# Grouped-query attention on one core: five of sixteen exps on VectorE, one of them as a pair summed on GpSimd

## The chip, the core and the metric

The kernel runs on one core of a Trainium2 chip. The core has engines that run side by side, each with its own queue of instructions: TensorE (PE, matrix multiplications, with its weight loads shown as PEld), VectorE (DVE), ScalarE (ACT), GpSimd (POOL) and SyncE (SP, which here only issues transfers). An instruction starts when those ahead of it on its engine have been issued and the semaphores it waits for are reached. Matrix products land in PSUM, eight banks of 2 KB per partition; everything else lies in SBUF. The metric is the device time of one execution in microseconds.

## The reference

Attention with 32 query heads and 8 key/value heads, batch 8, sequence 512, head size 64; four query heads share one key/value head.

```python
Q = Q.transpose(0, 2, 1, 3)
K_expanded = K_expanded.transpose(0, 2, 1, 3)
V_expanded = V_expanded.transpose(0, 2, 1, 3)
scores = np.einsum('bhqd,bhkd->bhqk', Q, K_expanded) * scale
weights = np.exp(scores - np.max(scores, axis=-1, keepdims=True))
weights = weights / (np.sum(weights, axis=-1, keepdims=True) + 1e-10)
output = np.einsum('bhqk,bhkd->bhqd', weights, V_expanded)
return output.transpose(0, 2, 1, 3).astype(np.float32)
```

## The kernel before

A unit is one batch entry and two key/value heads with their eight query heads; there are 32. A unit has 16 score tiles, four for each of four pairs of query heads. One score tile (`mm_scores`) is two matmuls of 64x128 weights against 64x512 queries, the two halves of the array at work on one head each, into a tile of two PSUM banks. There are three such slots, so PE can be ahead of the exps by three tiles. Two further banks, the x tiles, serve transposes and output blocks in turn.

The exps have no maximum subtracted. Most run on ACT (`exp_act`, one instruction for 128x1024). Some run on DVE (`exp_dve`): the score is multiplied and shifted so that, converted to a 16-bit integer, its bits are those of a bf16 number near the exponential (Schraudolph's method). The table `TILES` marks by a 1 the tiles of a unit that go to DVE, four of sixteen here. A 2 marks a tile whose bits go to a tile `lo` instead; GpSimd then makes a second copy `hi`, half an octave up (64 added to each 16-bit number), and adds the two as bf16 into the probability tile `pt`, so that the errors of the two approximations partly cancel. In the kernel before no tile is marked 2.

The output (`mm_out`) is made in blocks of four matmuls, 128 keys each, with V and a column of ones, so that column 64 of a block holds the sum of the weights. A unit has 32 blocks; DVE copies them out of PSUM in groups (`take_out`, tile `raw`). When a unit is whole, DVE takes the reciprocal of the sums, GpSimd multiplies (`divide`), and SP stores. Q, K and V are loaded as bf16 by GpSimd's queue; K and Q are transposed by PE (`mm_turn`) and copied out by DVE (`take_turn`, tiles `kt` and `qt`), and two transfers on SP make a copy of `kt` with its halves swapped, which the second head of a score tile needs.

The order of all this is written out ahead by the class `Plan`, with a cost for each kind of work. `SCORES` says for each of 16 places in a unit whether the score tile made there is one for ACT or for DVE; `FILL` says how many blocks or transposes PE does after each place; `ORDER` is the sequence of these (K4 the four transposes of K, 08 and 18 eight transposes of the first and the second half of Q, o7 seven output blocks); `SKIP` shifts that sequence against the places. The output blocks of a unit are made while the next unit's scores are. DVE takes what is ready first by the plan's costs. `fix` is the time that the plan allows for the work on GpSimd behind a tile marked 2.

```python
TILES = [int(c) for c in "0100010001000100"]
SCORES = "ADAADAADAAADAAAA"
FILL = [0, 0, 13, 0, 0, 7, 0, 0, 6, 0, 7, 0, 4, 0, 0, 15]
ORDER = "o4 o7 K4 08 18 o7 o7 o7".split()
```

Of the kernel before, what the change touches and what calls it, by code (L numbers as in the profile page):

```python
# [11 lines left out]
BF16 = mybir.dt.bfloat16  # L12
U8 = mybir.dt.uint8
U16 = mybir.dt.uint16
PE = mybir.EngineType.PE
ACT = mybir.EngineType.Activation
DVE = mybir.EngineType.DVE
# [5 lines left out]
class Plan:  # L23
# [11 lines left out]
    SCH, SCH_VIS = 1.14, 1.277  # L35
    DRAIN = 0.1

    def __init__(self, nu, tiles, scores, fill, groups, skip, arrive, x_cost, fix, nslot, nx, npt):
        self.ops = []
        qa = [16 * u + t for u in range(nu) for t in range(16) if not tiles[t]]  # L40
        qd = [16 * u + t for u in range(nu) for t in range(16) if tiles[t]]
        pt, pair_done, parts = {}, {}, {(0, None): 0.0, (0, 0): 0.0}
        slots, xs = [0.0] * nslot, [0.0] * nx
        ready = []
        self.pe = self.act = self.dve = 0.0
        ia = id_ = gi = at = nxt = 0
        scoring = False
        carry = -skip

        def run_dve(until):  # L50
            while ready:
                j = min(ready, key=lambda j: (max(j[0] - self.dve, 0.0), j[0]))
                start = max(self.dve, j[0])
                if start > until:
                    return
                ready.remove(j)
                self.ops.append((start, "dve", j[1], j[2]))
                if j[1] == "score":
                    cost, vis = self.SCH, self.SCH_VIS
                    slots[j[3]] = start + vis  # L60
                    pt[j[2]] = start + vis + (fix if tiles[j[2] % 16] == 2 else 0.0)
                else:
                    cost, vis = x_cost(j[2])
                    xs[j[3]] = start + vis
                    if j[1] == "turn":
                        swap = 4.0 if j[2][2] is None else 0.0
                        parts[j[2][1:3]] = start + vis + swap
                self.dve = start + cost

        def step_dve():  # L70
            assert ready
            run_dve(min(max(self.dve, j[0]) for j in ready) + 1e-9)

        def known(d, key):
            while d[key] >= NEVER if isinstance(d, list) else key not in d:
                step_dve()
            return d[key]

        for u in range(nu + 3):
            for k in range(16):  # L80
                at_dve = scores[k] == "D"
                if (id_ < len(qd)) if at_dve else (ia < len(qa)):
                    t = qd[id_] if at_dve else qa[ia]
                    p = t // 4
                    start = self.pe + (0.0 if scoring else self.DRAIN)
                    run_dve(start)
                    start = max(start, known(parts, (p // 4, None)), known(parts, (p // 4, p % 4 // 2)))
                    assert p < npt or p - npt in pair_done
                    while True:
                        s = min(range(nslot), key=lambda i: slots[i])  # L90
                        if ready and min(max(self.dve, j[0]) for j in ready) < max(start, slots[s]):
                            step_dve()
                        elif slots[s] >= NEVER:
                            step_dve()
                        else:
                            break
                    self.pe = max(start, slots[s])
                    scoring = True
                    slots[s] = NEVER
                    self.ops.append((self.pe, "pe", "score", (t, s)))  # L100
                    if at_dve:
                        ready.append((self.pe + self.SCORE_LAT, "score", t, s))
                        id_ += 1
                    else:
                        start = max(self.act, self.pe + self.SCORE_LAT)
                        self.ops.append((start, "act", "score", t))
                        self.act = start + self.EXP
                        slots[s] = pt[t] = start + self.EXP_VIS
                        ia += 1
                    self.pe += self.SCORE  # L110
                carry += fill[k]
                loose = u < 1 or u >= nu - 2
                while carry > 0 and gi < len(groups):
                    f = groups[gi]
                    start = self.pe + (self.DRAIN if scoring else 0.0)
                    run_dve(start)
                    limit = start + 0.1 if loose and u < nu else NEVER
                    if at == 0:
                        while xs[nxt % nx] >= NEVER:
                            step_dve()  # L120
                        start = max(start, xs[nxt % nx])
                    if f[0] == "turn":
                        start = max(start, arrive(f))
                    else:
                        p = f[1] * 4 + (f[2] + at) // 8
                        if p * 4 + 3 >= 16 * nu or any(
                            t not in pt and t not in [j[2] for j in ready if j[1] == "score"]
                            for t in range(4 * p, 4 * p + 4)
                        ):
                            assert loose  # L130
                            break
                        start = max([start] + [known(pt, t) for t in range(4 * p, 4 * p + 4)])
                    if start > limit:
                        break
                    self.pe = start
                    scoring = False
                    self.ops.append((start, "pe", f[0], (f, at)))
                    self.pe += self.TURN if f[0] == "turn" else self.BLOCK
                    carry -= 1
                    if at == 0:  # L140
                        x = nxt % nx
                        xs[x] = NEVER
                        nxt += 1
                    at += 1
                    if f[0] == "out" and (f[2] + at) % 8 == 0:
                        pair_done[p] = self.pe
                    if at == f[3]:
                        ready.append((self.pe + self.X_LAT, f[0], f, x))
                        gi, at = gi + 1, 0
                carry = min(carry, 16)  # L150
        run_dve(NEVER)
        assert ia == len(qa) and id_ == len(qd) and gi == len(groups)
        self.ops = [o for _, o in sorted(enumerate(self.ops), key=lambda e: (e[1][0], e[0]))]
# [3 lines left out]
def kernel(  # L157
# [7 lines left out]
    nc = tc.nc  # L165

    B, S, H, D = Q.shape
# [11 lines left out]

    TILES = [int(c) for c in "0100010001000100"]
    SCORES = "ADAADAADAAADAAAA"
    FILL = [0, 0, 13, 0, 0, 7, 0, 0, 6, 0, 7, 0, 4, 0, 0, 15]
    ORDER = "o4 o7 K4 08 18 o7 o7 o7".split()
    SKIP = 9

    scale = 1.0 / math.sqrt(D)
    A_schr = (2.0 ** 7) / math.log(2.0) * scale
# [82 lines left out]
    def exp_dve(t):  # L272
# [11 lines left out]
        )  # L284
        if two:
            high = two_pool.tile([128, 2, S], U16, name="hi")
            nc.gpsimd.tensor_scalar(
                out=high, in0=bits, scalar1=HALF_OCTAVE, scalar2=None, op0=mybir.AluOpType.add
            )
            nc.gpsimd.tensor_tensor(  # L290
                out=dst, in0=bits.bitcast(BF16), in1=high.bitcast(BF16), op=mybir.AluOpType.add
# [18 lines left out]
    def take_out(f, now):  # L310
# [11 lines left out]
        for a, b in ((0, 2 * BLK), (2 * BLK, 3 * BLK)) if last else (  # L322
            (0, 2 * BLK), (2 * BLK, UB)
        ) if u == NU - 2 else ((0, UB),):
            if lo < b <= lo + n:
                divide(u, a, b - a, nc.vector if last and a else nc.gpsimd)
                wait = 4.5 if b - a == UB else 2.8
                later.append((now + wait, lambda a=a, b=b: store(u, a, b - a, nc.sync)))

    def divide(u, lo, n, eng, src=None):  # L330
        src = raws[u][:, lo:lo + n, :] if src is None else src
        inv = inv_pool.tile([128, UB], FP32, name="inv")[:, 0:n]
        nc.vector.reciprocal(out=inv, in_=src[:, :, D])  # L333
        nh = n // SC
        eng.tensor_tensor(  # L335
            out=osbs[u].rearrange("p qc h d -> p h qc d")[:, lo // SC:lo // SC + nh],
            in0=src[:, :, 0:D].rearrange("p (h qc) d -> p h qc d", h=nh),
            in1=inv.rearrange("p (h qc) -> p h qc", h=nh)[:, :, :, None].to_broadcast(
                (128, nh, SC, D)
            ),  # L340
            op=mybir.AluOpType.mult,
        )

    def store(u, lo, n, eng):
        b, gp = divmod(u, GP)
# [33 lines left out]
                load_q(u + 3)  # L379

    turned = {}
    groups = [("turn", 0, 1, 8), ("turn", 1, None, 4), ("turn", 1, 0, 8), ("turn", 1, 1, 8)]
    for u in range(NU - 1):
        lo = 0
        for word in ORDER:
# [16 lines left out]
    def arrive(f):  # L402
        return {(0, 1): 0.5, (1, None): 3.0}.get(f[1:3], 6.0 if f[1] == 1 else 0.0)

    plan = Plan(
        NU, TILES, SCORES, FILL, groups, SKIP, arrive, x_cost,
        fix=5.0, nslot=NSLOT, nx=2, npt=6,
    )

    with tc.manual_schedule(engines={PE, ACT, DVE, POOL, SP}):  # L410
# [13 lines left out]
        v1f = first.tile([128, SC, 2, D1], BF16, name="v1f")  # L424
        nc.gpsimd.memset(v1f[:, :, :, D:D1], 1.0)
        v1[0] = v1f
        load_q(0, lo=HPG)
        load_k(0)
        load_q(1)
# [85 lines left out]
```

## Time and profile before

| | |
|---|---|
| time, median of 3 runs | 370.14 us (369.25 to 370.32) |
| profiled execution | 370.1 us, its span 368.2 us |
| ACT busy | 355.6 us, 97% |
| PE busy (ends modelled) | 341.9 us, 93% |
| DVE busy | 304.2 us, 83% |
| POOL busy | 167.1 us, 45% |
| DMA | 64.41 MB, mean 175 GB/s |
| granted TensorE clock | 0.995 |

The span runs from the first to the last instruction in the trace. A busy share is an average over the span; a busy time counts an instruction until its result has landed, and the next one on the engine can begin a little earlier, so that summed times can exceed what the engine needs. In the rows of the timeline stand start, duration, engine, line, operation, output and input tiles, and in brackets how long the engine was idle ahead of it and what ended that.

### The profile page before, as it was taken

What the parts mean: (1) busy time and instruction counts of PE and PEld (TensorE: products, weight loads), DVE (VectorE), ACT (ScalarE), POOL (GpSimd) and SP (SyncE); (2) the same over time, 40 slices, a digit from 0 to 9 for tenths busy, and PEclk for the clock granted to TensorE, in tenths of its full rate; (3) what the DMA queues carried; (4) which work ended last, traced back from release to release, by engine and by line L of the source; (5) the groups of instructions that cost most, each with busy time, mean ns of one, the idle gap of its engine ahead of it and who ended that gap; (6) DMA issues with size and microseconds to landing.
All of it is one profiled execution on the core that took longest, in us unless ns stands there. A gap on an engine that the chain in (4) does not pass through costs nothing.

```text
span 368.2 us, 13048 instructions
## 1 busy us (share of the span) xinstructions
PE 341.9 (93%) x5774; PEld 220.6 (60%) x5774; DVE 304.2 (83%) x430; ACT 355.6 (97%) x387; POOL 167.1 (45%) x105
## 2 busy tenths in 40 slices
PE   8799999999999999999999999999999999999993
PEld 3366566666565666566656566656666656666652
DVE  3788888888888888888888888898888898988883
ACT  4999999999999999999999999999999999999993
POOL 5334642446444264642436454254643436333161
PEclk9999999999999999999999999999999999999998
DMA  8999667797669966698865967879657995712355
GB/s 186 207 204 208 147 127 173 141 254 224 138 123 230 247 158 154 140 207 206 188 169 94 255 176 173 187 168 261 162 113 162 213 264 143 169 55 98 129 202 144
DMA packets 51480, 64.41 MB, mean 175 GB/s; under 512 B 3424, under 2 KB 36064, under 8 KB 51424
## 3 DMA queue, kind: packets, MB, share of 16 engines
q0 software_dynamic: 25344, 24.91, 42.8%
q1 hardware_dynamic: 25024, 38.28, 33.0%
q8 instruction: 45, 0.74, 0.8%
q10 hardware_dynamic: 1056, 0.39, 0.4%
q14 instruction: 11, 0.09, 0.1%
HBM read 50.86 MB, written 33.55 MB: 229 GB/s over the span
## 4 chain that ended last, share of the span: by engine, by line
PE 47%; ACT 34%; DVE 12%; DMA 2%; issue 2%; POOL 0%; ACTq 0%; DVEq 0%; POOLq 0%
ACT pt L265 34%; PE x L301 27%; DVE pt L277 11%; DMA k_nat<-in_K_dram 2%; DVE raw L321 0%; PE x L362 0%; DVE o_sb L335 0%; POOL q_nat L222 0%; ACTq L265 0%; PE s_2568 L254 0%; DVEq L277 0%; DVE inv L333 0%; PE s_344 L254 0%; PE s_6778 L254 0%; PE s_6531 L254 0%
## 5 line engine op out<-in xcount | busy, mean ns | idle before, releaser
L335 POOL TENSOR_TENSOR o_sb<-raw,inv 128x2048 f32<-128x2048 f32 (+1 forms) x33 | 114.1, 3458 | 183.4 <-issue 135.8
L301 PEld LDWEIGHTS <-pt 128*128 128x128 bf16 x4096 | 134.3, 98 | 40.2 <-issue 39.4
L321 DVE COPY raw<-x 128x455 f32<-128x455 f32 (+1 forms) x161 | 93.5, 581 | 45.7 <-PE x L301 45.7
L254 PEld LDWEIGHTS <-kt 64*128 64x128 bf16 x1024 | 51.1, 93 | 81.1 <-issue 54.8
L376 DVE COPY qt<-x 128x1024 bf16<-128x1024 bf16 x63 | 42.9, 681 | 0.7 <-PE x L362 0.7
L362 PE MATMUL x<-ident,q_nat 128*128 128x128 bf16 x504 | 39.2, 220 | 0.1
L362 PEld LDWEIGHTS <-q_nat 128*128 128x128 bf16 x504 | 28.3, 98 | 15.6 <-issue 15.2
L222 POOL DMA_DIRECT2D q_nat<-in_Q_dram x32 | 25.6, 801 | 0.1
L301 PE MATMUL x<-v_6732,pt 128*128 128x65 bf16 x512 | 18.9, 194 | 0.8 <-ACT pt L265 0.7
L301 PE MATMUL x<-v_5749,pt 128*128 128x65 bf16 x512 | 19.0, 194 | 0.0
L301 PE MATMUL x<-v_2800,pt 128*128 128x65 bf16 x512 | 19.0, 194 | 0.0
L301 PE MATMUL x<-v_3783,pt 128*128 128x65 bf16 x512 | 19.0, 194 | 0.0
L301 PE MATMUL x<-v_1817,pt 128*128 128x65 bf16 x512 | 19.0, 194 | 0.0
L301 PE MATMUL x<-v_4766,pt 128*128 128x65 bf16 x512 | 19.0, 194 | 0.0
L301 PE MATMUL x<-v_834,pt 128*128 128x65 bf16 x512 | 19.0, 194 | 0.0
L301 PE MATMUL x<-v_182,pt 128*128 128x65 bf16 x384 | 14.2, 194 | 0.0
L369 DVE COPY kt<-x 128x512 bf16<-128x512 bf16 x31 | 12.8, 414 | 0.0
L333 DVE RECIPROCAL inv<-raw 128x32 f32<-128x32 f32 (+2 forms) x34 | 11.6, 341 | 1.2
L362 PE MATMUL x<-ident,k_nat 128*128 128x128 bf16 x124 | 12.2, 219 | 0.4 <-DMA k_nat<-in_K_dram 0.4
L362 PEld LDWEIGHTS <-k_nat 128*128 128x128 bf16 x124 | 7.4, 97 | 1.0 <-DMA k_nat<-in_K_dram 0.5
L234 POOL DMA_DIRECT2D v_nat<-in_V_dram x8 | 6.1, 761 | 0.0
L229 POOL DMA_DIRECT2D k_nat<-in_K_dram x8 | 6.0, 751 | 0.0
(1068 smaller groups left out, 809.1 us busy)
## 6 DMA issues: line engine op xcount, KB each, us to landing
out_dram<-o_sb SPq DMA_DIRECT2D x30, 1024.0 KB, 5.6
q_nat<-in_Q_dram POOLq DMA_DIRECT2D x31, 512.0 KB, 8.4
k_nat<-in_K_dram POOLq DMA_DIRECT2D x8, 512.0 KB, 10.5
v_nat<-in_V_dram POOLq DMA_DIRECT2D x8, 512.0 KB, 12.4
kt<-kt SPq DMA_DIRECT2D x62, 64.0 KB, 2.0
out_dram<-o_sb SPq DMA_DIRECT2D x3, 512.0 KB, 3.8
q_102<-in_Q_dram ACTq DMA_DIRECT2D x1, 256.0 KB, 4.4
k_103<-in_K_dram SPq DMA_DIRECT2D x1, 256.0 KB, 3.9
```

The costliest lines, as they stand in the source:

```text
L222: nc.gpsimd.dma_start(out=t[:, :, lo * D:], in_=rows(Q, b, HU * gp + lo, HU * (gp + 1)))
L234: nc.gpsimd.dma_start(out=t, in_=rows(V, b, 0, KV))
L254: nc.tensor.matmul(s[:, m, :], kt[u][64 * m:64 * m + 64, 0 if m == g else 1, kc * 128:(kc + 1) * 128], qt[u][64 * m:64 * m + 64, i, :], st ...
L265: nc.scalar.activation(out=pts[p][:, kc, :, :], in_=score.pop(t), func=mybir.ActivationFunctionType.Exp, scale=float(scale),)
L277: nc.vector.tensor_scalar(out=bits, in0=score.pop(t), scalar1=float(A_schr), scalar2=float(B_two if two else B_one), op0=mybir.AluOpType.mult,
L301: nc.tensor.matmul(xs[f][:, at * D1:(at + 1) * D1], pts[u * HPG + i][:, kc, m, qc * 128:(qc + 1) * 128], v1[u][:, kc, 2 * i // HPG, :], st ...
L321: nc.vector.tensor_copy(out=raws[u][:, lo:lo + n, :], in_=x[:, 0:n * D1])
L333: nc.vector.reciprocal(out=inv, in_=src[:, :, D])
L335: eng.tensor_tensor(out=osbs[u].rearrange("p qc h d -> p h qc d")[:, lo // SC:lo // SC + nh], in0=src[:, :, 0:D].rearrange("p (h qc) d -> ...
L362: nc.tensor.transpose(xs[f][:, at * 128:(at + 1) * 128], src, ident)
L369: nc.vector.tensor_copy(out=k[:, 0, :], in_=x[:, 0:S])
L376: nc.vector.tensor_copy(out=qt[u][:, 2 * part:2 * part + 2, :], in_=x)
```

## The change

One more tile of each unit goes to DVE, as a pair (the 2 in `TILES`, tile 11); the tables of the order are new, with K's transposes first; `hi` is made by an add of 32-bit integers, each holding two 16-bit numbers, against a constant tile `shift`; a whole unit's division is made in two halves; and some constants of the plan differ.

```diff
-    TILES = [int(c) for c in "0100010001000100"]
-    SCORES = "ADAADAADAAADAAAA"
-    FILL = [0, 0, 13, 0, 0, 7, 0, 0, 6, 0, 7, 0, 4, 0, 0, 15]
-    ORDER = "o4 o7 K4 08 18 o7 o7 o7".split()
-    SKIP = 9
+    TILES = [int(c) for c in "0100010001020100"]
+    SCORES = "DAADAADAAADAADAA"
+    FILL = [0, 8, 0, 0, 13, 0, 0, 8, 0, 0, 9, 6, 0, 0, 8, 0]
+    ORDER = "K4 o7 08 o7 o6 18 o7 o5".split()
+    SKIP = 21
...
             high = two_pool.tile([128, 2, S], U16, name="hi")
-            nc.gpsimd.tensor_scalar(
-                out=high, in0=bits, scalar1=HALF_OCTAVE, scalar2=None, op0=mybir.AluOpType.add
+            nc.gpsimd.tensor_tensor(
+                out=high.rearrange("p m s -> p (m s)").bitcast(I32),
+                in0=bits.rearrange("p m s -> p (m s)").bitcast(I32),
+                in1=shift,
+                op=mybir.AluOpType.add,
             )
...
-                wait = 4.5 if b - a == UB else 2.8
+                wait = 5.0 if b - a == UB else 2.8
                 later.append((now + wait, lambda a=a, b=b: store(u, a, b - a, nc.sync)))
...
-        nh = n // SC
-        eng.tensor_tensor(
-            out=osbs[u].rearrange("p qc h d -> p h qc d")[:, lo // SC:lo // SC + nh],
...
+        parts = 2 if n == UB else 1
+        for part in range(parts):
+            nh = n // SC // parts
+            h0 = nh * part
+            eng.tensor_tensor(
+                out=osbs[u].rearrange("p qc h d -> p h qc d")[:, lo // SC + h0:lo // SC + h0 + nh],
...
-    groups = [("turn", 0, 1, 8), ("turn", 1, None, 4), ("turn", 1, 0, 8), ("turn", 1, 1, 8)]
+    groups = [("skip", 2), ("turn", 0, 1, 8), ("skip", 4), ("turn", 1, None, 4)]
+    groups += [("skip", SKIP - 6), ("turn", 1, 0, 8), ("turn", 1, 1, 8)]
...
-        fix=5.0, nslot=NSLOT, nx=2, npt=6,
+        fix=6.0, nslot=NSLOT, nx=2, npt=6,
...
+        shift = const.tile([128, S], I32)
+        nc.gpsimd.memset(shift, HALF_OCTAVE * 0x10001)
```

In the class `Plan` a group of the kind `skip` takes the place of the single number at the start, and the allowance for the swapped copy of `kt` is 6.0 instead of 4.0 (3.0 for the second unit).

On DVE, one unit in the middle of the program before; the names are output and input tile, `s_` the score tiles:

```order
L333 RECIPROCAL inv<-raw 128x32
L321 COPY raw<-x 128x260
L321 COPY raw<-x 128x455
L369 COPY kt<-x 128x512
L277 TENSOR_SCALAR pt<-s_4034 128x1024
L376 COPY qt<-x 128x1024
L277 TENSOR_SCALAR pt<-s_4068 128x1024
L376 COPY qt<-x 128x1024
L277 TENSOR_SCALAR pt<-s_4105 128x1024
L321 COPY raw<-x 128x455 x2
L277 TENSOR_SCALAR pt<-s_4179 128x1024
L321 COPY raw<-x 128x455
```

and a unit of the changed one, from its first exp to its fifth; a copy of 325 elements and the reciprocal follow and close it:

```order
L284 TENSOR_SCALAR pt<-s_3808 128x1024
L382 COPY kt<-x 128x512
L331 COPY raw<-x 128x455
L284 TENSOR_SCALAR pt<-s_3858 128x1024
L389 COPY qt<-x 128x1024
L284 TENSOR_SCALAR pt<-s_3906 128x1024
L331 COPY raw<-x 128x455
L331 COPY raw<-x 128x390
L284 TENSOR_SCALAR lo<-s_3958 128x1024
L389 COPY qt<-x 128x1024
L331 COPY raw<-x 128x455
L284 TENSOR_SCALAR pt<-s_4017 128x1024
```

The fourth exp writes `lo`; K's copy has moved behind the first exp, and the output copies stand between the exps one or two at a time, with 455, 455, 390, 455 and 325 elements.

On POOL, the loads and the division of two units before:

```order
L222 DMA q_nat<-in_Q_dram 128x4x512
L229 DMA k_nat<-in_K_dram 128x4x512
L234 DMA v_nat<-in_V_dram 128x4x512
L335 TENSOR_TENSOR o_sb<-raw,inv 128x8x4x64
L222 DMA q_nat<-in_Q_dram 128x4x512
L335 TENSOR_TENSOR o_sb<-raw,inv 128x8x4x64
```

and of the change, from the copy of V that one unit in four has:

```order
L247 COPY v_3812<-v_nat 128x32x64
L294 TENSOR_TENSOR hi<-lo,shift 128x512
L300 TENSOR_TENSOR pt<-lo,hi 128x1024
L229 DMA q_nat<-in_Q_dram 128x4x512
L348 TENSOR_TENSOR o_sb<-raw,inv 128x4x4x64 x2
```

The shift and the sum stand ahead of the Q load and of the unit's two half divisions, on one queue with them.

On PE, the place in the changed program where the sum is waited for, inside a run of output blocks:

```order
L311 LDWEIGHTS pt
L311 MATMUL x<-v_2809,pt 128x65
L311 LDWEIGHTS pt [waits Pool_49]
L311 MATMUL x<-v_2809,pt 128x65
L311 LDWEIGHTS pt
```

The fourth matmul of a block, the one with the tile's keys, holds the wait; all that PE does afterwards, scores too, stands behind it. Before, PE waits for POOL in this way only at a new batch entry's V.

More of the change, by code (lines that the diff above doesn't have):

```diff
@@ L14 @@
 U16 = mybir.dt.uint16
+I32 = mybir.dt.int32
 PE = mybir.EngineType.PE
@@ L36, with __init__ @@
     DRAIN = 0.1
-    def __init__(self, nu, tiles, scores, fill, groups, skip, arrive, x_cost, fix, nslot, nx, npt):
+    def __init__(self, nu, tiles, scores, fill, groups, arrive, x_cost, fix, nslot, nx, npt):
         self.ops = []
@@ L47, in __init__ @@
         scoring = False
-        carry = -skip
+        carry = 0
         def run_dve(until):
@@ L65, in run_dve @@
                     if j[1] == "turn":
-                        swap = 4.0 if j[2][2] is None else 0.0
+                        swap = 0.0 if j[2][2] is not None else 3.0 if j[2][1] == 1 else 6.0
                         parts[j[2][1:3]] = start + vis + swap
@@ L114, in __init__ @@
                     f = groups[gi]
+                    if f[0] == "skip":
+                        step = min(carry, f[1] - at)
+                        carry, at = carry - step, at + step
+                        if at == f[1]:
+                            gi, at = gi + 1, 0
+                        continue
                     start = self.pe + (self.DRAIN if scoring else 0.0)
@@ L333, in divide @@
         nc.vector.reciprocal(out=inv, in_=src[:, :, D])
-        nh = n // SC
-        eng.tensor_tensor(
-            out=osbs[u].rearrange("p qc h d -> p h qc d")[:, lo // SC:lo // SC + nh],
[L337 to L342, printed above, removed]
+        parts = 2 if n == UB else 1
[4 more added lines that the diff above has]
+                out=osbs[u].rearrange("p qc h d -> p h qc d")[:, lo // SC + h0:lo // SC + h0 + nh],
+                in0=src[:, :, 0:D].rearrange("p (h qc) d -> p h qc d", qc=SC)[:, h0:h0 + nh],
+                in1=inv.rearrange("p (h qc) -> p h qc", qc=SC)[:, h0:h0 + nh, :, None].to_broadcast(
+                    (128, nh, SC, D)
+                ),
+                op=mybir.AluOpType.mult,
+            )
     def store(u, lo, n, eng):
@@ L405 @@
     plan = Plan(
-        NU, TILES, SCORES, FILL, groups, SKIP, arrive, x_cost,
-        fix=5.0, nslot=NSLOT, nx=2, npt=6,
+        NU, TILES, SCORES, FILL, groups, arrive, x_cost,
+        fix=6.0, nslot=NSLOT, nx=2, npt=6,
     )
```

## The prediction

> **What bounds the kernel now.** I read the busy shares, the chain that ended last, one stretch by engine, then the timeline of one unit (16 score tiles; 32 units in all).
>
> ```profile
> span 368.2 us, 13048 instructions
> ...
> PE 341.9 (93%) x5774; PEld 220.6 (60%) x5774; DVE 304.2 (83%) x430; ACT 355.6 (97%) x387; POOL 167.1 (45%) x105
> ...
> PE 47%; ACT 34%; DVE 12%; DMA 2%; issue 2%; POOL 0%; ACTq 0%; DVEq 0%; POOLq 0%
> ```
>
> The chain names PE first, but it is not PE's own work that sets the pace; ACT is the full engine. The stretches from 72 to 336 us repeat each other, four units in 44 us:
>
> ```profile
> 72.00:116.00 44.00, 41.87 (x720) 27.35 (x720) 37.61 (x53) 44.00 (x50) 20.87 (x12) 1.00 0.83 194
> ```
>
> The columns are length, busy time of PE, weight loads, DVE, ACT and POOL, then granted clock (1.00), DMA share and GB/s. ACT is never empty; DVE is idle for 6.4 us of 44, POOL for more than half. One unit lasts 11.02 us, from one reciprocal to the next:
>
> ```profile
> 182.78 0.35 DVE L333 RECIPROCAL inv<-raw 128x32 f32<-128x32 f32 x1
> ...
> 193.80 0.35 DVE L333 RECIPROCAL inv<-raw 128x32 f32<-128x32 f32 x1
> ```
>
> and ACT starts an exp every 0.90 us, except where its score comes late:
>
> ```profile
> 188.58 1.11 ACT L265 ACTIVATE pt<-s_4098 128x1024 bf16<-128x1024 f32 x1
> ...
> 189.48 1.12 ACT L265 ACTIVATE pt<-s_4109 128x1024 bf16<-128x1024 f32 x1
> ...
> 189.99 0.39 PE L254 MATMUL s_4139<-qt,kt 64*128 64x512 bf16 x2
> ...
> 190.47 1.05 ACT L265 ACTIVATE pt<-s_4139 128x1024 bf16<-128x1024 f32 x1
> ```
>
> The score at 189.99 is read 0.48 later, 0.09 after ACT could have begun. Twelve exps at 0.905 are 10.86; some 0.15 of such late scores make the 11.01. So the bound is ACT plus 1.4%.
>
> **The change, part by part.** Three engines must be costed for a new unit.
>
> ACT: eleven exps at 0.905 = 9.96, a loss of 0.905 per unit.
>
> DVE: one exp more; the output copies are cut 7, 7, 6, 7, 5 blocks instead of 4, 7, 7, 7, 7, the two Q copies, the K copy and the reciprocal stay. What one instruction costs DVE is read from start to next start, where nothing else held it:
>
> ```profile
> 182.13 0.62 DVE L321 COPY raw<-x 128x455 f32<-128x455 f32 x1
> ...
> 183.56 0.43 DVE L321 COPY raw<-x 128x260 f32<-128x260 f32 x1 [0.43 <-PE x L301]
> ...
> 184.35 0.63 DVE L321 COPY raw<-x 128x455 f32<-128x455 f32 x1 [0.35 <-PE x L301]
> ...
> 184.90 0.41 DVE L369 COPY kt<-x 128x512 bf16<-128x512 bf16 x1
> ...
> 185.23 1.21 DVE L277 TENSOR_SCALAR pt<-s_4034 128x1024 uint16<-128x1024 f32 x1
> ...
> 188.17 0.68 DVE L376 COPY qt<-x 128x1024 bf16<-128x1024 bf16 x1
> ...
> 188.81 1.23 DVE L277 TENSOR_SCALAR pt<-s_4105 128x1024 uint16<-128x1024 f32 x1
> ...
> 189.95 0.62 DVE L321 COPY raw<-x 128x455 f32<-128x455 f32 x1
> ```
>
> An exp 1.14 (188.81 to 189.95), a 455-element copy 0.55 (184.35 to 184.90), K 0.33: each its duration less 0.08. By that rule Q is 0.60, the reciprocal 0.27, and a 390-element copy, between 0.43 for 260 and 0.63 for 455, 0.48. The 325-element copy takes 0.50, and the reciprocal, which reads it, follows 0.03 after its end (182.13 + 0.62 to 182.78): 0.53. Sum: 5 x 1.14 + 3 x 0.55 + 0.48 + 0.53 + 0.27 + 0.33 + 2 x 0.60 = 10.16. The old unit by the same pitches is 9.0.
>
> PE: nothing is added, and the work is in six runs between scores, as before.
>
> ```profile
> 184.47 0.39 PE L254 MATMUL s_4031<-qt,kt 64*128 64x512 bf16 x2
> 184.69 0.38 PE L254 MATMUL s_4034<-qt,kt 64*128 64x512 bf16 x2
> ...
> 185.16 0.39 PE L254 MATMUL s_4042<-qt,kt 64*128 64x512 bf16 x2
> ...
> 185.48 0.90 PE L362 MATMUL x<-ident,q_nat 128*128 128x128 bf16 x13
> ...
> 186.31 0.39 PE L254 MATMUL s_4062<-qt,kt 64*128 64x512 bf16 x2
> ...
> 190.53 1.04 PE L301 MATMUL x<-v_2800,pt 128*128 128x65 bf16 x28
> ...
> 191.50 0.39 PE L254 MATMUL s_4179<-qt,kt 64*128 64x512 bf16 x2
> ```
>
> A score tile is 0.22; a score before other work 0.32, so a switch costs 0.10; 13 transposes with a switch 0.83, so 0.056 each; 28 output matmuls with one 0.97, so 0.124 for four. A unit: 16 x 0.22 + 32 x 0.124 + 20 x 0.056 + 12 x 0.10 = 9.81. K's four transposes only move to the unit's start, their DVE copy behind the first exp; both swap DMAs on SP move with them and stay ahead of the unit's store. This K serves the next unit, some 8.5 us after the copy, and a swap lands in 2.0:
>
> ```profile
> kt<-kt SPq DMA_DIRECT2D x62, 64.0 KB, 2.0
> ```
>
> The planner's new constants and the store's later place only set the order. So that part costs nothing; if a swap came late, its lateness would stand in every unit before the first score.
>
> So DVE becomes the longest with 10.16. Does the order let it run without holes? The score slots are the danger. An exp frees its slot 1.27 after its start, ACT's 1.07:
>
> ```profile
> 180.99 1.22 DVE L277 TENSOR_SCALAR pt<-s_3935 128x1024 uint16<-128x1024 f32 x1
> ...
> 182.26 0.39 PE L254 MATMUL s_3967<-qt,kt 64*128 64x512 bf16 x2 [0.26 <-DVE pt L277]
> ```
>
> ```profile
> 15.82 1.02 ACT L265 ACTIVATE pt<-s_264 128x1024 bf16<-128x1024 f32 x1
> ...
> 16.89 0.39 PE L254 MATMUL s_280<-qt,kt 64*128 64x512 bf16 x2 [0.47 <-ACT pt L265]
> ```
>
> Counted from the unit's first DVE exp, the five start at 0, 2.02, 3.76, 5.93 and 8.22 if DVE never waits. The third and the next unit's first use the slot of the DVE exp before them: 2.02 + 1.27 + 0.47 = 3.76, just in time; 8.22 + 1.27 + 0.47 = 9.96 against 10.16, 0.2 to spare. Walked through in the same way, the other scores wait for an ACT exp by at most 0.2, which PE's spare 0.35 per unit takes up, and each copy finds its matmuls done with 0.1 to 0.4 in hand. The weave closes, but with no more room than the old one had; I give it the same 0.15 of late arrivals: 10.3 per unit.
>
> POOL: the pair adds two instructions, and the division in halves two launches for one. None of the new forms is in the trace. The nearest rows:
>
> ```profile
> L335 POOL TENSOR_TENSOR o_sb<-raw,inv 128x2048 f32<-128x2048 f32 x30 | 108.4, 3614 | 180.3 <-issue 134.3 <-DVE inv L333 46.0
> ...
> L222 POOL DMA_DIRECT2D q_nat<-in_Q_dram x32 | 25.6, 801 | 0.1
> ...
> L335 POOL TENSOR_TENSOR o_sb<-raw,inv 128x1024 f32<-128x1024 f32 x3 | 5.7, 1901 | 3.0 <-issue 1.5 <-DVE inv L333 0.8 <-POOL o_sb L335 0.7
> ...
> L240 POOL COPY v_834<-v_nat 128x2048 bf16<-128x2048 bf16 x1 | 1.9, 1882 | 0.0
> ```
>
> Two-input elements cost 1.67 ns each and 0.19 a launch (2048 against 1024): the shift on 512 words 1.05, the sum on 1024 1.90, together 2.95. At the rate of the one-input bf16 copy, 0.92 ns, it would be 1.4. Upward the rows set no end; 5.9 stands for twice the estimate. I take 2.95, since both new instructions have two inputs. POOL per unit is then 3.80 (two halves) + 0.80 (Q load) + 0.92 (a quarter of the V copy, its memset, and the K and V issues) + 2.95 = 8.5 of 10.3: hidden. The sum is wanted late: PE reads that tile in the next unit, in the run after its eighth score tile, by the walk 8.5 after the DVE exp began; 1.3 for the exp and 2.95 leave 4.3. Behind the sum on POOL's queue wait the Q load, wanted some two units later, and the division, with three raw buffers. If this cover goes, every 1 us past the 4.3 stops PE for 1 us.
>
> By the Trainium skill (GPSIMD Engine Reference, "Performance versus the Vector engine") a two-input element takes about 2.6 cycles at 1.2 GHz and ordinary elementwise work is wrongly placed on that engine. By that the pair would be an estimated 3.3 us, still under its cover; the trace disagrees on the rate, since its 2048-element division took 3.61 where the page has 4.50 for an add.
>
> Start: the first tile goes to DVE, so ACT's first exp moves behind a transpose of Q.
>
> ```profile
> 7.08 0.78 PE L254 MATMUL s_170<-qt,kt 64*128 64x512 bf16 x2
> ...
> 7.90 1.03 ACT L265 ACTIVATE pt<-s_170 128x1024 bf16<-128x1024 f32 x1 [0.86 <-PE s_170 L254]
> ...
> 8.82 1.02 ACT L265 ACTIVATE pt<-s_186 128x1024 bf16<-128x1024 f32 x1
> ```
>
> ACT starts near 8.82, where its second exp was; with ACT's usual lag of 1.17 behind a unit's first score that is 0.6 more than a steady unit. End: the last score stood 7.8 before the end of the span (368.2 - 360.44).
>
> ```profile
> 360.44 0.39 PE L254 MATMUL s_7957<-qt,kt 64*128 64x512 bf16 x2
> ```
>
> Now 64 output matmuls follow it instead of 48 (0.5 more, of which ACT's last exp hides some: 0.3), and the last pair is met at once: about 4.6 after its exp's score where PE arrives after 3.8, and with a division in front of it on POOL 1 us: 9.1.
>
> Sum: 7.1 + 0.6 + 32 x 10.3 + 9.1 = 346.4 span. The profiled execution took 370.1 for its 368.2, so 1.9 lie around it; its time equals the median of 370.14. Forecast: 348.
>
> **The rivals.** *The weave slips (0.23).* Three slots and two x tiles tie PE, ACT and DVE, at 9.8, 9.96 and 10.16, so a late arrival on one no longer falls into another's idle time. Before, ACT paid about 0.08 at two places; if DVE pays it at each of the six runs, a unit is 10.65, and the time 16.8 + 32 x 10.65 + 1.9 = 359. For it: a spare of nothing at the third exp. Against it: the old order held its full engine to 1.4%.
>
> *POOL's pair is dear (0.06), the slower side.* POOL has 5.5 per unit beside the pair; from a pair of 5.5 the unit exceeds the old 11.02, POOL is the bound, PE stands at the matmul that waits for the sum, and at 6.5 the unit is 12.0: 16.8 + 384 + 1.9 = 403. For it: no such instruction has a row. Against: it needs twice the rate of the division.
>
> *K or V comes late (0.03).* K is loaded by POOL and turned earlier in the order.
>
> ```profile
> k_nat<-in_K_dram POOLq DMA_DIRECT2D x8, 512.0 KB, 10.5
> ```
>
> Issued when the division ends, about 5 into a batch's second unit, it lands at 16 and is wanted at 19.6 (the end of the third). If the queue took 2 us longer than that at all seven changes of batch: 348 + 14 = 362.
>
> *Nothing gained (0.02).* If a longer wait replaced all of ACT's 0.9, a unit would stay at 11.0: 371.
>
> *Better than the walk (0.04):* 10.16 with nothing lost, and the end's pair wait not met: 342.
>
> **How the numbers follow.** The forecast has 0.62, with 10.2 to 10.45 a unit, 344 to 353. The range for 8 in 10 reaches into the slipped weave: 343 to 360. 0.3%, 1.1 us, is about what a measurement of this kernel can tell from no change. Faster: 0.62 + 0.23 + 0.03 + 0.04 = 0.92; same 0.02; slower 0.06.
>
> **What would show it.** Right: units of 10.3 from reciprocal to reciprocal, DVE busy above 95% in a middle stretch, ACT with gaps of 0.3 to 0.4 a unit, a shift near 1.05 and a sum near 1.9, and no wait of PE for POOL outside the last unit. Wrong: PE waiting for POOL in every unit, POOL full, DVE with holes behind the second exp, or transposes waiting for K's load.

## The result

The changed kernel takes 354.32 us (median of 4 runs, 353.92 to 354.67), against 370.11 before on the same chip: a ratio of 0.958, with a 95% interval of 0.956 to 0.960. The forecast was 348 with a range of 343 to 360. The direction and most of the size came out; 6 us of the forecast gain did not come.

The page of the profiled execution, first the span and the busy shares, then the chain that ended last:

```profile
span 352.3 us, 13157 instructions
...
PE 337.3 (96%) x5774; PEld 227.6 (65%) x5774; DVE 333.0 (95%) x462; ACT 333.3 (95%) x355; POOL 279.9 (79%) x200
...
PE 75%; ACT 17%; DVE 2%; POOL 1%; issue 1%; DMA 1%; ACTq 0%; DVEq 0%; POOLq 0%
```

Three engines now stand at 95 to 96%. DVE, which the prediction made the longest, has 2% of the chain, and PE with ACT has 92%. The stretches of four units show the same loads (columns: length, PE, weight loads, DVE, ACT, POOL, granted clock, DMA share, GB/s):

```profile
72.00:116.00 44.00, 43.65 (x758) 29.86 (x758) 43.20 (x60) 43.57 (x47) 37.29 (x26) 1.00 0.86 192
```

DVE has gone from 37.6 of 44 to 43.2, POOL from 20.9 to 37.3, ACT is no longer quite full. A unit, from one reciprocal to the next in the timeline:

```profile
91.31 0.35 DVE L343 RECIPROCAL inv<-raw 128x32 f32<-128x32 f32 x1
...
101.73 0.35 DVE L343 RECIPROCAL inv<-raw 128x32 f32<-128x32 f32 x1
...
112.16 0.35 DVE L343 RECIPROCAL inv<-raw 128x32 f32<-128x32 f32 x1
```

is 10.43 where it was 11.02. From the first unit's reciprocal (28.67) to the thirtieth's (331.36) the mean is 10.44.

**Where the other 6 us are.** The forecast span was 346.4; it is 352.3. The units are 10.44 instead of 10.3 (32 x 0.14 = 4.5). The start cost 1.15 over 32 such units where 0.6 was set down, and began 0.3 earlier. The end, from the last score (342.04) to the end of the span, took 10.3 instead of 9.1 (1.2 more). Together that is the 5.9.

The order around the unit's critical place in the timeline, PE's scores and ACT's exps in order of time, one view for each engine:

```profile
99.35 0.39 PE L261 MATMUL s_2256<-qt,kt 64*128 64x512 bf16 x2
99.58 0.38 PE L261 MATMUL s_2260<-qt,kt 64*128 64x512 bf16 x2
99.93 0.39 PE L261 MATMUL s_2264<-qt,kt 64*128 64x512 bf16 x2
...
101.37 0.38 PE L261 MATMUL s_2303<-qt,kt 64*128 64x512 bf16 x2
101.82 0.39 PE L261 MATMUL s_2307<-qt,kt 64*128 64x512 bf16 x2
...
103.38 0.38 PE L261 MATMUL s_2350<-qt,kt 64*128 64x512 bf16 x2
103.65 0.39 PE L261 MATMUL s_2357<-qt,kt 64*128 64x512 bf16 x2
...
105.14 0.39 PE L261 MATMUL s_2392<-qt,kt 64*128 64x512 bf16 x2
...
107.22 0.38 PE L261 MATMUL s_2449<-qt,kt 64*128 64x512 bf16 x2
107.61 0.39 PE L261 MATMUL s_2454<-qt,kt 64*128 64x512 bf16 x2
...
108.61 0.39 PE L261 MATMUL s_2477<-qt,kt 64*128 64x512 bf16 x2
...
109.78 0.39 PE L261 MATMUL s_2509<-qt,kt 64*128 64x512 bf16 x2
```

```profile
98.82 1.06 ACT L272 ACTIVATE pt<-s_2224 128x1024 bf16<-128x1024 f32 x1
99.83 1.02 ACT L272 ACTIVATE pt<-s_2256 128x1024 bf16<-128x1024 f32 x1
100.75 1.02 ACT L272 ACTIVATE pt<-s_2264 128x1024 bf16<-128x1024 f32 x1
101.66 1.03 ACT L272 ACTIVATE pt<-s_2299 128x1024 bf16<-128x1024 f32 x1
102.56 1.04 ACT L272 ACTIVATE pt<-s_2307 128x1024 bf16<-128x1024 f32 x1
...
105.62 1.02 ACT L272 ACTIVATE pt<-s_2392 128x1024 bf16<-128x1024 f32 x1
106.54 1.02 ACT L272 ACTIVATE pt<-s_2402 128x1024 bf16<-128x1024 f32 x1
```

Read them as one path. The score at 99.35 is read by ACT 0.48 later; ACT, with its pace of 0.905 from 98.82, had been free for 0.1. Three more exps follow in ACT's own pace; the last, begun at 102.56, frees its slot 1.09 later, and exactly then, at 103.65, PE makes the score that waited for it. Behind this score stand eight transposes and five output blocks; then comes the score of 105.14, which ACT, idle by now, reads at 105.62. The exp after that, of 106.54, frees its slot 1.07 later, at 107.61, where PE again has just been waiting. Two runs on PE lead to the score of 109.78, one unit after 99.35. In order the pieces are 0.48 + 2.73 + 1.09 + 1.49 + 0.48 + 0.92 + 1.07 + 1.00 + 1.17 = 10.43: ACT's pace and PE's runs in turn, closed by the three score slots. Nobody is idle for long, and DVE is not on it.

The same rows give PE's waits for a slot. A score follows the score before it after 0.22 where nothing holds it; those at 99.93, 101.82, 103.65 and 107.61 come after 0.35, 0.45, 0.27 and 0.39, so they waited 0.13, 0.23, 0.05 and 0.17, together 0.58. Each comes 1.07 to 1.11 after the start of an ACT exp (98.82, 100.75, 102.56, 106.54), the time in which such an exp frees its slot.

### The profile page after: what moved, and what is told of

It reads as the page before. It is cut to its first block, busy times and chain, and to the rows that moved or that the text cites. A ratio compares the mean times of both kernels' runs of the same rounds, so it can differ in the third digit from the quotient of the medians.

```text
span 352.3 us, 13157 instructions
## 1 busy us (share of the span) xinstructions
PE 337.3 (96%) x5774; PEld 227.6 (65%) x5774; DVE 333.0 (95%) x462; ACT 333.3 (95%) x355; POOL 279.9 (79%) x200
## 4 chain that ended last, share of the span: by engine, by line
PE 75%; ACT 17%; DVE 2%; POOL 1%; issue 1%; DMA 1%; ACTq 0%; DVEq 0%; POOLq 0%
PE x L311 32%; ACT pt L272 17%; PE x L375 11%; DMA q_102<-in_Q_dram 1%; DVE pt L284 1%; POOL pt L300 1%; DVE raw L331 0%; POOL hi L294 0%; PE x L461 0%; POOL o_sb L348 0%; DVE inv L343 0%; DVE q_105 L467 0%; ACTq L272 0%; ACT q_105 L454 0%; DVE qt L389 0%
## 5 line engine op out<-in xcount | busy, mean ns | idle before, releaser
L311 PEld LDWEIGHTS <-pt 128*128 128x128 bf16 x4096 | 138.4, 98 | 25.4 <-issue 23.4
L348 POOL TENSOR_TENSOR o_sb<-raw,inv 128x1024 f32<-128x1024 f32 x63 | 118.7, 1908 | 1.9 <-DVE inv L343 1.3
L261 PEld LDWEIGHTS <-kt 64*128 64x128 bf16 x1024 | 56.9, 93 | 66.0 <-issue 37.4
L331 DVE COPY raw<-x 128x455 f32<-128x455 f32 (+3 forms) x161 | 90.1, 577 | 2.9 <-PE x L311 2.2
L294 POOL TENSOR_TENSOR hi<-lo,shift 128x512 int32<-128x512 int32 x32 | 40.6, 1269 | 52.1 <-DVE lo L284 52.1
L300 POOL TENSOR_TENSOR pt<-lo,hi 128x1024 bf16<-128x1024 bf16 x32 | 68.0, 2124 | 2.5
L311 PE MATMUL x<-v_6821,pt 128*128 128x65 bf16 x512 | 19.5, 194 | 1.8 <-POOL pt L300 1.7
L311 PE MATMUL x<-v_3812,pt 128*128 128x65 bf16 x512 | 19.6, 194 | 0.0
L311 PE MATMUL x<-v_5818,pt 128*128 128x65 bf16 x512 | 19.6, 194 | 0.0
L311 PE MATMUL x<-v_1806,pt 128*128 128x65 bf16 x512 | 19.6, 194 | 0.0
L311 PE MATMUL x<-v_4815,pt 128*128 128x65 bf16 x512 | 19.6, 194 | 0.0
L311 PE MATMUL x<-v_803,pt 128*128 128x65 bf16 x512 | 19.6, 194 | 0.0
L311 PE MATMUL x<-v_2809,pt 128*128 128x65 bf16 x512 | 19.6, 194 | 0.0
L375 PE MATMUL x<-ident,k_nat 128*128 128x128 bf16 x124 | 17.2, 222 | 0.2 <-DMA k_nat<-in_K_dram 0.2
L311 PE MATMUL x<-v_181,pt 128*128 128x65 bf16 x384 | 14.7, 194 | 0.0
L375 PEld LDWEIGHTS <-k_nat 128*128 128x128 bf16 x124 | 8.7, 97 | 7.3 <-issue 6.8
```

Source lines behind the costliest of these rows:

```text
L261: nc.tensor.matmul(s[:, m, :], kt[u][64 * m:64 * m + 64, 0 if m == g else 1, kc * 128:(kc + 1) * 128], qt[u][64 * m:64 * m + 64, i, :], st ...
L294: nc.gpsimd.tensor_tensor(out=high.rearrange("p m s -> p (m s)").bitcast(I32), in0=bits.rearrange("p m s -> p (m s)").bitcast(I32), in1=shift,
L300: nc.gpsimd.tensor_tensor(out=dst, in0=bits.bitcast(BF16), in1=high.bitcast(BF16), op=mybir.AluOpType.add)
L311: nc.tensor.matmul(xs[f][:, at * D1:(at + 1) * D1], pts[u * HPG + i][:, kc, m, qc * 128:(qc + 1) * 128], v1[u][:, kc, 2 * i // HPG, :], st ...
L331: nc.vector.tensor_copy(out=raws[u][:, lo:lo + n, :], in_=x[:, 0:n * D1])
L348: eng.tensor_tensor(out=osbs[u].rearrange("p qc h d -> p h qc d")[:, lo // SC + h0:lo // SC + h0 + nh], in0=src[:, :, 0:D].rearrange("p (h ...
```

## The experiments

Two theories of the unit stood against each other: that of the prediction (DVE, with 10.16 of work, sets it, plus some late arrivals), and the circuit through PE, ACT and the slots, which I call C.

**1. DVE's work shortened.**

```diff
-nc.vector.tensor_copy(out=qt[u][:, 2 * part:2 * part + 2, :], in_=x)
+nc.vector.tensor_copy(out=qt[u][:, 2 * part, :], in_=x[:, 0:S])
-                qt[u][64 * m:64 * m + 64, i, :],
+                qt[u][64 * m:64 * m + 64, i - i % 2, :],
```

> Edit: DVE copies only half of each transposed Q block out of PSUM, and the scores of the second head pair of each half use the first's queries, so a part of the scores is left out; DVE's work falls by 2 x 0.27 = 0.53 us per unit, PE, ACT and GpSimd keep theirs. Theory of the prediction (DVE is the longest engine and sets the unit): the unit falls from 10.43 towards ACT's 9.96, time 340 to 346. Theory C (a circuit through PE and ACT sets the unit and DVE only has holes): less than 1.5 us of change, 353 to 355.

Measured: 353.88 us, ratio to before 0.959 (0.955 to 0.963), as without the edit. The stretch of four units:

```profile
72.00:116.00 44.00, 43.65 (x760) 29.79 (x756) 41.05 (x60) 43.53 (x48) 37.34 (x26) 1.00 0.86 192
```

DVE is busy 41.05 instead of 43.20, all else is the same to a tenth, and the mean unit is 10.44 in both. So DVE's load did not set the unit.

**2. ACT's exps shortened.**

```diff
-            out=pts[p][:, kc, :, :],
-            in_=score.pop(t),
+            out=pts[p][:, kc, :, 0:480],
+            in_=score.pop(t)[:, :, 0:480],
...
-                pts[u * HPG + i][:, kc, m, qc * 128:(qc + 1) * 128],
+                pts[u * HPG + i][:, kc, m, min(qc * 128, 352):min(qc * 128, 352) + 128],
```

> Edit: each exp on ACT makes 960 of its 1024 columns (the last output block of a head reads columns 352 to 480 instead of 384 to 512, so a part of the weights is left out); each is shorter by about 0.055 us, ACT's unit by 0.6. Theory C (six ACT durations and the PE runs between them close the circuit of 10.43): 6 x 0.055 = 0.33 less per unit until DVE's own 10.07 to 10.16 is met, 344 to 347. Theory of the prediction (DVE sets the unit): less than 2 us of change, 352 to 354.

Measured: 345.77 us, ratio 0.935 (0.934 to 0.937), as theory C has it.

```profile
89.29 0.35 DVE L343 RECIPROCAL inv<-raw 128x32 f32<-128x32 f32 x1
...
99.43 0.35 DVE L343 RECIPROCAL inv<-raw 128x32 f32<-128x32 f32 x1
```

The unit fell by 0.27 in the mean (0.29 in the one shown), about five times the 0.055 taken from one exp; the circuit, with six, would have given 0.33, up to the next bound.

**3. PE's runs shortened.**

```diff
-        for kc in range(SC):
+        for kc in range(1, SC):
...
-                start=(at == 0 and kc == 0),
+                start=(at == 0 and kc == 1),
```

> Edit: each output block is made of three matmuls instead of four (the first 128 keys are left out of the output); PE's unit falls by 32 x 0.031 = 1.0 us. Theory C: the three PE runs in the circuit hold 12 blocks, 12 x 0.031 = 0.37 less per unit until DVE's 10.07 to 10.16 is met, 342 to 346. Theory of the prediction (DVE sets the unit, PE has 0.35 to spare already): less than 2 us of change, 352 to 354.

Measured: 347.72 us, ratio 0.940 (0.939 to 0.942). PE's work is on the circuit too, as C has it; the time is 1.7 above C's range, since the units stop at 10.21, a fall of 0.2 where C had 0.37.

```profile
72.00:116.00 44.00, 41.78 (x649) 26.48 (x646) 43.39 (x60) 43.86 (x49) 37.75 (x26) 1.00 0.87 196
```

DVE's rows have few holes there, so its 10.16 may be the next bound; no run tests that.

**4. DVE and ACT shortened together.** Both edits above in one kernel.

> Edit: the halved Q copies on DVE and the 960 columns on ACT together (both leave out a part, as in their own runs). With ACT short alone the unit was 10.13, and DVE's instructions stood there without holes. If DVE's 10.16 was then the bound: taking 0.53 from it lets the unit fall until PE's 9.8 with its waits, 9.85 to 10.0, time 337 to 341. If PE's density was the bound there: no further change, 345 to 346.

Measured: 345.74 us, ratio 0.934 (0.932 to 0.935), the same as with ACT short alone. I had read DVE's rows in experiment 2, which stood there without holes, as the next bound. They were not. The chain here gives PE nine tenths:

```profile
PE 90%; DVE 3%; ACT 3%; DMA 1%; POOL 1%; issue 1%; DVEq 0%; POOLq 0%
```

I read this as PE's own 9.8 with some 0.3 of waits for slots, about 10.1, behind the circuit through ACT, and DVE only behind that. That order is read from the rows; no run shortens ACT and PE together.

**5. The kernel before with ACT's exps shortened.** The edit of experiment 2 on the old kernel: was ACT alone its bound?

> Edit: the kernel before, with each exp on ACT making 960 of 1024 columns (a part of the weights is left out, as in the same edit of the changed kernel). ACT's unit falls by 12 x 0.055 = 0.66. If ACT alone set the old unit, as the prediction read it (12 x 0.905 and 0.15 of late scores): the unit falls to 10.35, 347 to 351. If the same kind of circuit through the three slots, PE and ACT already stood close behind ACT's full load: the unit stops at 10.8 to 10.9, 363 to 367.

Measured: 365.68 us, ratio 0.988 (0.986 to 0.989). ACT's unit became 0.66 shorter; the kernel's became about 0.15 shorter.

```profile
82.70 0.35 DVE L333 RECIPROCAL inv<-raw 128x32 f32<-128x32 f32 x1
...
93.55 0.35 DVE L333 RECIPROCAL inv<-raw 128x32 f32<-128x32 f32 x1
```

```profile
PE 68%; DVE 24%; DMA 3%; issue 3%; ACT 2%; POOL 0%; DVEq 0%; POOLq 0%
```

So the old order had its own path through PE and DVE just behind ACT's full load, at 10.86. An ACT that was busy all the time was a bound, but one with 0.15 per unit below it. To take an exp from ACT was worth little until the tables of the order also let the rest go faster.

**6. K's transposes first, alone.**

```diff
-    ORDER = "o4 o7 K4 08 18 o7 o7 o7".split()
+    ORDER = "K4 o4 o7 08 18 o7 o7 o7".split()
```

> Edit: the kernel before, with only K's transposes put first in a unit (the order K4 o4 o7 08 18 o7 o7 o7 instead of o4 o7 K4 08 18 o7 o7 o7). The prediction gave this step no cost and no gain: 369 to 371. If the order of PE's runs against the exps sets the unit (theory C), the old table no longer fits it: slower, 372 to 378.

Measured: 375.17 us, ratio 1.014 (1.012 to 1.016); a unit is 11.13 to 11.16. The step that the prediction had at nothing costs 5 us in the old tables: no work is added, and I read the loss as PE's runs falling elsewhere between the exps. What the step is worth within the new tables no run shows.

**7. The division in halves, alone,** on the kernel before (the loop over `parts` of the diff).

> Edit: the kernel before, with only the whole unit's division on GpSimd made in two halves. The prediction gave it 0.19 us more on GpSimd per unit, under cover: 369.5 to 371, no change. If GpSimd's launches or their place in its queue mattered: a change of 1 us or more.

Measured: 370.37 us, ratio 1.001 (1.000 to 1.002): no change, as expected.

**8. No pair on GpSimd.**

```diff
-        two = TILES[t % len(TILES)] == 2
+        two = False
```

> Edit: the tile marked 2 is made on DVE alone, with the single approximation, so GpSimd's shift and sum are left out (and with them the pair's accuracy); every table and the order of the other engines stay. Theory A (the pair lies under other work except at the end, where PE waited 1.7 us for it): units stay at 10.43 us, the end is shorter by 1.7 to 2, about 352.5. Rival B (GpSimd's two instructions per unit slow something in every unit, by a shared resource or by lateness): units shorter by 0.1 or more, 349 or less.

Measured: 352.84 us, ratio 0.954 (0.953 to 0.956); the units stay at 10.43. Theory A: GpSimd's part lies under other work all along, and costs about 1.5 us at the very end. There the changed kernel's waits have one row for it:

```profile
PE x L311 <- POOL pt L300: 1.7, 1, 1.7
```

(engine, what it waited for, us in total, times, longest).

**9. No pair in the last unit only.**

```diff
-        two = TILES[t % len(TILES)] == 2
+        two = TILES[t % len(TILES)] == 2 and t < 16 * (NU - 1)
```

> Edit: only in the last unit the tile marked 2 is made on DVE alone, without GpSimd's pair (a little less accurate for that one unit's tiles). Theory A (GpSimd's pair costs time only at the end): the same gain as with no pair anywhere, 1.4 to 1.8 us, about 352.8, ratio to before 0.954. If the pair cost something in every unit, only part of that gain: 353.5 or more.

Measured: 352.73 us, ratio 0.9535 (0.952 to 0.955). The whole of what the pair cost comes back from one unit, and this version beats both kernels.

**10. GpSimd's sum made twice.** A loop of two around the sum into `dst`.

> Edit: GpSimd adds the pair twice, 2.1 us more in each unit, nothing else changes. PE reads the tile some 4.2 us after the sum is ready, so by lateness alone nothing is lost but 2.1 at the end: 356 to 357 (theory L). By GpSimd's throughput: a unit on it becomes 1.36 + 2 x 2.12 + 0.83 + 3.77 + 0.93 = 11.1, more than 10.43, so it becomes the bound: 31 x 0.67 + 2 more, 375 to 378 (theory T, the slower side of the prediction).

Measured: 372.85 us, ratio 1.0075 (1.0055 to 1.009), slower than before the change; below the forecast of 375 to 378, but far from 357. Stretch and waits:

```profile
160.00:204.00 44.00, 41.46 (x720) 28.16 (x719) 41.24 (x57) 41.19 (x45) 43.28 (x29) 1.00 0.80 181
```

```profile
PE x L312 <- POOL pt L301: 18.4, 14, 4.7
```

POOL is full (43.3 of 44), and PE waits for it in 14 units, up to 4.7 us at a time; a unit is 10.9 in the mean. What ends the cover is GpSimd's load per unit, not how late one sum is: 2.1 us more would have fitted into the 4.2 us of slack of one tile.

**11. The shifted copy with 16-bit numbers**, as it stood in the code before: `tensor_scalar` on 1024 of them instead of `tensor_tensor` on 512 words.

> Edit: the shifted copy is made as before the change, 1024 16-bit numbers plus a constant, instead of 512 32-bit words plus a constant tile. By the one-input copy of V (0.92 ns an element) it takes 1.0 to 1.1 us instead of 1.27; by the two-input rate 1.9 or more. Under theory A neither moves the time by more than what it adds or takes at the end: 353.9 to 355.5.

Measured: 355.88 us, ratio 0.963 (0.960 to 0.965), 0.4 above the range I gave, and the instruction itself far outside what the rows had suggested. The group of this kernel and that of the changed one:

```profile
L294 POOL TENSOR_SCALAR hi<-lo 128x1024 uint16<-128x1024 uint16 x32 | 88.7, 2773 | 6.2 <-DVE lo L284 6.0
```

```profile
L294 POOL TENSOR_TENSOR hi<-lo,shift 128x512 int32<-128x512 int32 x32 | 40.6, 1269 | 52.1 <-DVE lo L284 52.1
L300 POOL TENSOR_TENSOR pt<-lo,hi 128x1024 bf16<-128x1024 bf16 x32 | 68.0, 2124 | 2.5
```

2.77 us against 1.27. POOL is then nearly full and the units still hold 10.43:

```profile
72.00:116.00 44.00, 43.65 (x765) 30.03 (x762) 43.18 (x60) 43.62 (x47) 43.30 (x26) 1.00 0.85 191
```

Its busy time, 43.3 of 44, is that of experiment 10, where PE waits in 14 units; here PE waits for it once. A busy share of 98% does not tell a load that just fits from one that does not. Here the difference shows at the end, where PE waits 3.3 instead of 1.7. So the 32-bit add is worth 1.6 us in the time, and 1.5 us of GpSimd in every unit, which is what keeps it from the place of experiment 10.

**12. Other tables,** with the edit of experiment 9. Walked through by hand, these tables make the circuit 0.03 shorter.

```diff
-    TILES = [int(c) for c in "0100010001020100"]
-    FILL = [0, 8, 0, 0, 13, 0, 0, 8, 0, 0, 9, 6, 0, 0, 8, 0]
-    ORDER = "K4 o7 08 o7 o6 18 o7 o5".split()
+    TILES = [int(c) for c in "0001200111000000"]
+    FILL = [0, 8, 0, 0, 13, 0, 0, 8, 0, 0, 10, 5, 0, 1, 6, 1]
+    ORDER = "K4 o7 08 o6 o7 18 o7 o5".split()
```

> Edit: the changed kernel without the pair in its last unit (as in the run of that edit), and with tables that put one more block into the run behind the eleventh score and spread the last run (FILL ends 10, 5, 0, 1, 6, 1, the DVE tiles are 3, 4 as the pair, 7, 8 and 9, o6 and o7 change places). Walking the circuit through PE and ACT gives 10.42 per unit instead of 10.45 and about 0.5 less at the end: 351.3 to 352.2 (theory C, little left in the tables). If the unit were bound by DVE, which has the same work in both: as without the pair in the last unit, 352.7.

Measured: 354.12 us, ratio 0.956 (0.954 to 0.9575): slower than experiment 9, against either expectation. The middle units are 10.43 like the others, but one is 10.76 and the last of them 10.53, and the first reciprocal comes 0.65 later (29.50 against 28.85). Why those units slip stays open.

## Why the prediction was right, and where not

- *What bounds the kernel before.* Half right. ACT was full and a unit was its twelve exps plus 0.15; but experiment 5 shows the next bound 0.15 below, on a path of PE and DVE. The reading of a full engine did not show how little lay behind it.
- *The new loads.* ACT's 9.96 needs no correction: its pace is still 0.90 to 0.92. DVE's 10.16 fits: in experiment 2, where ACT was short, its instructions ran almost without holes at 10.14 a unit.
- *DVE becomes the longest, and the unit is 10.16 plus 0.15.* This is the step that failed. The prediction said that the other scores wait for an ACT exp by at most 0.2, "which PE's spare 0.35 per unit takes up". The waits are of about that size (the longest is 0.23), but a spare at one place does not pay for a wait at another: between the waits lie PE's runs, and behind them ACT runs dry. These pieces add up around the unit to 10.43. Nor is it enough that the longest single wait is below the spare: the waits of the unit shown are 0.58 in sum, and all are for ACT. Experiments 1, 2 and 3 show it: shortening DVE gives nothing, shortening ACT or PE gives 6 to 9 us. A fourth score slot, the direct test of the ring, was not run; all eight PSUM banks are in use. The third exp of DVE, named as the place without room, did slip (by 0.18), but as a result, not as the cause.
- *The time inside the range* is in part luck. The 0.15 of late arrivals was taken over from the old kernel and not worked out; 0.28 above DVE's 10.16 stood in its place, and from another cause. 354.3 lies past the 353 that the prediction gave its own mechanism, in the part of the range that it added for the slipped weave. One of its signs of being right misled: DVE is busy 98% of the middle stretch, as it said, without setting the pace. Another held: PE has one wait for POOL's sum, in the last unit.
- *The rival of the slipped weave* had the place nearly right (three slots tie the engines together) and the wrong engine as the payer; its 10.65 was too much.
- *POOL's pair is hidden.* Right, and the 4.3 us of slack stood (4.2 between the sum's end and the matmul that reads it). The size was low: 1.27 and 2.12 instead of 1.05 and 1.90, 3.4 together. The estimate of 3.3 worked out from the Trainium skill (GPSIMD Engine Reference, "Performance versus the Vector engine") was nearer than the one from the division's rows. Its advice against such work on that engine did not decide here, where the engine had the time free (experiments 8 and 9).
- *The slower side.* It exists as described, through GpSimd's load per unit (experiment 10). The point from which it decides was put at a pair of 5.5; the run with about 5.6 is slower than before by 0.75%, though its unit is 10.9, not above 11.02: the rest lies at the start (first reciprocal at 30.12 instead of 28.54) and at the end.
- *K first costs nothing.* Not so in the old tables, where it costs 5 us (experiment 6); within the new ones it was not priced.
- *Start and end.* Both were under-estimated: 1.15 instead of 0.6, and 10.3 instead of 9.1, with 1.7 of the end the wait for the last pair that the prediction had at 1. The lag of 1.17 from which the start was reckoned has no row in the prediction; in the changed kernel it is 1.19 (101.37 to 102.56).

## What to carry to other kernels

Where engines hand buffers to each other in a ring, the longest engine's load is only a lower bound: follow one item round (score, exp, slot free, next score, the work queued behind it) and add up the pieces in the order in which they follow; a spare at one place of the ring does not pay for a wait at another. A quick test of which engine sets the pace is to shorten each one's work by some per cent in turn and see whether the time follows; do it on the kernel before as well, since a full engine may have the next bound just beneath it. Work moved to an engine off the path cost nothing here until its load per period was full, and then 18 us for 2.1 more per unit, so compare its sum per period, not only the slack of one item; what is hidden in every period may still stand open in the last one.

## What was not expected of the hardware

- On GpSimd the add of a constant to 1024 16-bit integers took 2.77 us, more than the sum of two bf16 tiles of the same size (2.12) and twice the add of 512 32-bit words with two inputs (1.27). The one-input bf16 copy of 2048 took 1.88 in the kernel before.
- The two 64 KB swap transfers of `kt` land after 5.0 us instead of 2.0. In the changed kernel a 512 KB load of Q is issued 1.2 us ahead of them on another queue (once 1.5, at 185.83 against 187.32); without the pair, where that load comes 2.4 to 4.3 us behind them, they land in 2.1. That the load is the cause is argued from this order, and the order is not all: in experiment 10, with the load 2.3 to 4.3 us behind, they take 3.0. It cost nothing that the units show: they are 10.43 with 5.0 and with 2.1.

```profile
kt<-kt SPq DMA_DIRECT2D x62, 64.0 KB, 5.0
```
